# A two-layer transformer trunk in fp32: rsqrt and q/k scaling on GpSimd, the first k copies on ScalarE's queue, two preparations at other places

## The chip, the cores and the metric

One core of a Trainium2 chip runs the whole program. The time is the device time of one execution in microseconds (us), and what is compared is the median over runs. Five engines work from their own in-order instruction queues: TensorE (PE in the profile; its weight loads are PEld), VectorE (DVE), ScalarE (ACT), GpSimd (POOL) and SyncE (SP), which only starts transfers. ScalarE and GpSimd can start transfers too. Engines wait for one another through semaphores.

## The reference

The input is 512 tokens by 1024 features. Two layers follow one another, each an attention and a SwiGLU feed-forward, all with RMSNorm in front and a residual sum behind. The parts that matter here:

```python
def rms_norm(x, g):
    y = xf * lax.rsqrt(jnp.mean(xf * xf, axis=-1, keepdims=True) + EPS)
    return (y * g.astype(jnp.float32)).astype(x.dtype)

# layer 0: 16 heads of 64, strictly causal
z = einsum('bqhd,bkhd->bhqk', q_blk, k) * scale
log_keep = where(earlier, log_sigmoid(-z), 0.0)
log_after = lax.cumsum(log_keep, axis=3, reverse=True) - log_keep
weight = where(earlier, exp(log_sigmoid(z) + log_after), 0.0)

# layer 1: 8 heads, each with two query/key halves of 64 and values of 128
q = rms_norm(q.reshape(b, s, 8, 2, 64), q_g);  k = rms_norm(k.reshape(b, s, 8, 2, 64), k_g)
q1, q2, k1, k2 = partial_rope(..., positions)          # the first 16 of 64 features are rotated
lam = exp(sum(lq1 * lk1)) - exp(sum(lq2 * lk2)) + lam_init
a = softmax(q1 k1) - lam * softmax(q2 k2)               # block-causal
o = rms_norm(a @ v, sub_g) * (1.0 - lam_init)

# after either attention
x = x + einsum('bse,ed->bsd', o, w_out)
x = x + (silu(h @ w_gate) * (h @ w_up)) @ w_down        # h = rms_norm(x, ffn_norm), 2816 wide
```

Everything is float32 in and out.

## The kernel before, in words

**Products.** Every big product runs as three passes over a high and a low part (`mm3`, L215 to L218): high times high, high times low, low times high. A weight tile of 128x1024 is loaded by SP into a raw tile (two of them, tag "raw"), ScalarE rounds it to the high part `whi` (L109) and VectorE subtracts to get the low part `wlo` (L110). There are five pairs of such buffers. In layer 0 the low part is instead made by ScalarE (`wlo` = minus `whi`, L120) and an adding transfer that GpSimd starts (L121). Layer 1's weights are split once during the first feed-forward and kept in device memory (`keep_split`, L126 to L131, transfers started by GpSimd), and layer 1 reads them back (L133 to L137).

**Norms.** x lies transposed, as eight tiles of 128 features by 512 tokens. `Norm.scaled` (L157) makes `hhi` on ScalarE and `hlo` on VectorE from a tile of x and the gain; `Norm.square` (L167) squares the tile on ScalarE (`sq`) and adds it to `ssum` on VectorE (L177). `tile_done` does both when a tile of x is final. `finish` (L183) sums over partitions with four small matmuls into `ps_ss`, takes the inverse root with three Newton steps on VectorE (`rsqrt`, L139 to L149: one starting instruction, then three times three), and spreads it over partitions by a matmul into `ps_bc`, which ScalarE copies to `rbc`. The factor is applied after the products that use `hhi` and `hlo`.

**Layer 0** (`stick_layer`, L390). The first q and k (`pq`, `pk`) are projected at once. `stack_k` (L328) splits k into a high and a low part and copies each 64-partition half to the other half by a transfer that GpSimd starts (L334), because `scores` (L337) reads high and low stacked. `weights` (L484) takes two sigmoids on ScalarE from each score bank, a running product on VectorE (the scan, L494) and a multiply (L502); TensorE transposes the result (L358). While a pair of heads is worked on, the projections of the next pair and of v are fed in between as fillers. The output projection then adds its banks to x (L284, L298), and each finished x tile calls `tile_done` of the feed-forward's norm.

**Feed-forward** (`ffn`, L572). The 22 column tiles of gate and up are done in three portions, each followed by its part of the down projection, in PSUM banks of a pool of six and a pool of two. After the first portion's down projection the first feed-forward calls `setup_diff` (L627): eight and more small transfers started by SP, some 70 small VectorE instructions, and ScalarE's exponentials and sines for layer 1's rotation tables and lambda. These buffers come from a pool of their own, so they depend on nothing in the feed-forward.

**Layer 1** (`diff_layer`, L711). For each of four chunks (two heads each) `qk_steps` (L754) projects q and k of all tokens, squares them, takes an inverse root of 128x32 sums (L771), scales 128x2048 values on VectorE (L773) and rotates them on GpSimd (L790 to L793). `head_stacks` transposes (`tqk`) and stacks them. `weights` (L806) is a softmax pair joined by one VectorE instruction (L828). `head_out` (L851) normalises a head's output: two transposes (`tn`, `tb`), squares (`o_sq`, L865) and an inverse root of 128x4 sums (L876) between them, on VectorE.

**Order.** Each engine's order is not the order of the code: a scheduler runs a simulated timeline of the program and places every instruction on its engine when its operands would be ready there. A change of one instruction's engine or duration therefore also moves others.

## Time and profile before

| what | value |
|---|---|
| median of three runs | 1266.99 us (1265.03 to 1267.15) |
| profiled execution | 1268.86 us; its span from first to last instruction 1267.0 us |
| TensorE busy | 1225.4 us, 97% of the span |
| VectorE, ScalarE, GpSimd busy | 732.2, 566.8 and 101.4 us |
| idle time of TensorE | 41.6 us |
| mean granted TensorE clock | 0.990 |

Busy time is summed over the whole span, so an engine with a small share may still be the one that is waited for at one place. The granted clock is a share of full speed: 1.00 is TensorE's upper level (2.4 GHz), 0.50 its lower one (1.2 GHz). In rows of a timeline the brackets give the idle time before the instruction and what ended it.

### The profile page before, as it was taken

What the parts mean: (1) busy time and instruction counts of PE and PEld (TensorE: products, weight loads), DVE (VectorE), ACT (ScalarE), POOL (GpSimd) and SP (SyncE); (2) the same over time, 40 slices, a digit from 0 to 9 for tenths busy, and PEclk for the clock granted to TensorE, in tenths of its full rate; (3) what the DMA queues carried; (4) which work ended last, traced back from release to release, by engine and by line L of the source; (5) the groups of instructions that cost most, each with busy time, mean ns of one, the idle gap of its engine ahead of it and who ended that gap; (6) DMA issues with size and microseconds to landing.
All of it is one profiled execution on the core that took longest, in us unless ns stands there. A gap on an engine that the chain in (4) does not pass through costs nothing.

```text
span 1267.0 us, 16005 instructions
## 1 busy us (share of the span) xinstructions
PE 1225.4 (97%) x5974; PEld 1024.5 (81%) x5974; DVE 732.2 (58%) x1396; ACT 566.8 (45%) x962; POOL 101.4 (8%) x169
## 2 busy tenths in 40 slices
PE   7899999989999999999999999987999999999998
PEld 6788888768888888888888998775888888888886
DVE  6467777677654555455633777885754434443442
ACT  7687977555432333233423555554442222222320
POOL 2211112001111111001101201100000000000000
PEclk9899999999999999999999999999999999999999
DMA  6966848236867776767645463531333233322222
GB/s 205 218 124 152 182 102 199 67 106 222 270 227 248 242 226 234 252 236 234 241 184 184 150 212 99 179 100 34 106 111 98 87 100 100 100 89 95 96 75 79
DMA packets 60397, 198.39 MB, mean 157 GB/s; under 512 B 8288, under 2 KB 9312, under 8 KB 60320
## 3 DMA queue, kind: packets, MB, share of 16 engines
q1 hardware_dynamic: 41760, 138.90, 34.3%
q0 software_dynamic: 18416, 58.47, 17.0%
q8 instruction: 47, 0.77, 0.2%
q14 instruction: 30, 0.25, 0.1%
q10 hardware_dynamic: 144, 0.01, 0.0%
HBM read 153.31 MB, written 35.65 MB: 149 GB/s over the span
## 4 chain that ended last, share of the span: by engine, by line
PE 89%; DVE 3%; issue 3%; DMA 3%; ACT 1%; POOL 0%; SPq 0%; DVEq 0%; POOLq 0%; ACTq 0%
PE ps_d L216 6%; PE ps_d L217 6%; PE ps_d L218 6%; PE ps_u L216 6%; PE ps_g L216 6%; PE ps_u L218 6%; PE ps_g L217 6%; PE ps_u L217 6%; PE ps_g L218 6%; PE ps_nat L216 4%; PE ps_nat L217 4%; PE ps_nat L218 4%; PE ps_o L216 2%; PE ps_o L217 2%; PE ps_o L218 2%
## 5 line engine op out<-in xcount | busy, mean ns | idle before, releaser
L109 ACT ACTIVATE whi<-wraw 128x1024 fp32r<-128x1024 f32 (+1 forms) x138 | 140.6, 1034 | 344.2 <-PE ps_d L217 82.4
L110 DVE TENSOR_TENSOR wlo<-wraw,whi 128x1024 fp32r<-128x1024 f32 (+1 forms) x138 | 164.2, 1191 | 93.7 <-ACT whi L109 47.5
L216 PE MATMUL ps_u<-hhi,whi 128*128 128x512 f32 x352 | 137.9, 392 | 3.5 <-DVE k L679 3.5
L217 PE MATMUL ps_d<-alo,whi 128*128 128x512 f32 x352 | 138.9, 396 | 0.0
L218 PE MATMUL ps_d<-ahi,wlo 128*128 128x512 f32 x352 | 138.9, 396 | 0.0
L216 PE MATMUL ps_d<-ahi,whi 128*128 128x512 f32 x352 | 138.7, 396 | 0.0
L216 PE MATMUL ps_g<-hhi,whi 128*128 128x512 f32 x352 | 137.5, 392 | 0.0
L218 PE MATMUL ps_u<-hhi,wlo 128*128 128x512 f32 x352 | 137.3, 390 | 0.0
L218 PE MATMUL ps_g<-hhi,wlo 128*128 128x512 f32 x352 | 137.2, 390 | 0.0
L217 PE MATMUL ps_g<-hlo,whi 128*128 128x512 f32 x352 | 137.1, 390 | 0.0
L217 PE MATMUL ps_u<-hlo,whi 128*128 128x512 f32 x352 | 137.0, 390 | 0.0
L216 PE MATMUL ps_nat<-whi,hhi 128*128 128x256 f32 (+1 forms) x384 | 124.1, 324 | 3.6 <-DVE k L457 3.0
L218 PE MATMUL ps_nat<-whi,hlo 128*128 128x256 f32 (+1 forms) x384 | 123.5, 322 | 0.0
L217 PE MATMUL ps_nat<-wlo,hhi 128*128 128x256 f32 (+1 forms) x384 | 122.9, 321 | 0.0
L610 DVE TENSOR_TENSOR x<-x,ps_d 128x512 f32<-128x512 f32 x48 | 32.8, 686 | 100.2 <-PE ps_d L218 100.2
L216 PEld LDWEIGHTS ps_nat<-whi,hhi 128*128 128x128 f32 x384 | 72.7, 190 | 11.0 <-DVE k L457 3.5
L216 PEld LDWEIGHTS ps_u<-hhi,whi 128*128 128x128 f32 x352 | 66.4, 189 | 17.9 <-issue 4.1
L218 PEld LDWEIGHTS ps_d<-ahi,wlo 128*128 128x128 f32 x352 | 66.1, 188 | 16.0
L216 PEld LDWEIGHTS ps_d<-ahi,whi 128*128 128x128 f32 x352 | 66.1, 188 | 16.0
L217 PEld LDWEIGHTS ps_d<-alo,whi 128*128 128x128 f32 x352 | 66.1, 188 | 15.9
L216 PEld LDWEIGHTS ps_g<-hhi,whi 128*128 128x128 f32 x352 | 66.4, 189 | 14.1 <-issue 0.2
L217 PEld LDWEIGHTS ps_g<-hlo,whi 128*128 128x128 f32 x352 | 66.2, 188 | 14.0 <-issue 0.2
(207 smaller groups left out, 2335.7 us busy)
## 6 DMA issues: line engine op xcount, KB each, us to landing
wraw<-in_wgu SPq DMA_DIRECT2D x88, 512.0 KB, 3.5
wraw<-in_wd SPq DMA_DIRECT2D x32, 512.0 KB, 3.6
k<-k POOLq DMA_DIRECT2D x32, 256.0 KB, 4.4
praw<-in_wqk SPq DMA_DIRECT2D x16, 512.0 KB, 5.1
kept_wqk<-whi POOLq DMA_DIRECT2D x16, 512.0 KB, 4.4
kept_wqk<-wlo POOLq DMA_DIRECT2D x16, 512.0 KB, 6.0
whi<-kept_wqk SPq DMA_DIRECT2D x16, 512.0 KB, 6.3
wlo<-kept_wqk SPq DMA_DIRECT2D x16, 512.0 KB, 6.2
```

What stands on the lines that cost most here:

```text
L109: A.activation(hi[:, :cols], raw[:, :cols], AF.Copy)
L110: V.tensor_tensor(lo[:, :cols], raw[:, :cols], hi.bitcast(F32)[:, :cols], op=ALU.subtract)
L216: T.matmul(ps, lh[0], rh[0], start=first, stop=False)
L217: T.matmul(ps, lh[0], rh[1], start=False, stop=False)
L218: T.matmul(ps, lh[1], rh[0], start=False, stop=last)
L610: V.tensor_tensor(x[m], x[m], ps, op=ALU.add)
```

## The change

Five edits:

1. The Newton steps of layer 1's inverse roots run on GpSimd (`rsqrt_pool`): the starting instruction stays on VectorE, and 13 GpSimd instructions follow, since each step takes four there instead of three. It is used for the q/k norm of all four chunks and for `head_out` of the first seven heads; the last head keeps VectorE (`final`). With it, two small multiplies per head move as well.
2. The 128x2048 scaling of q and k moves from VectorE (L773) to GpSimd (after: L810).
3. The first k copies of layer 0 are started from ScalarE's queue instead of GpSimd's.
4. The two feed-forward norms square their tiles only after the eighth tile is done, and the seven additions into `ssum` run on GpSimd (`early=False`).
5. `setup_diff` takes its buffers from a raw tile of the feed-forward's pool, which ties it to that pool's other users.

```diff
+    def rsqrt_pool(v, n):
...
+        V.tensor_scalar(
+            u.bitcast(I32), v.bitcast(I32), -0.5, RSQRT_MAGIC, op0=ALU.mult, op1=ALU.add
+        )
+        G.tensor_tensor(v, v, half.to_broadcast([P, n]), op=ALU.mult)
+        for _ in range(3):
+            G.tensor_tensor(t, u, u, op=ALU.mult)
+            G.tensor_tensor(t, t, v, op=ALU.mult)
+            G.tensor_tensor(t, t, c15.to_broadcast([P, n]), op=ALU.add)
+            G.tensor_tensor(u, t, u, op=ALU.mult)
+        return u
...
-        def square(self, i, eng=None):
+        def square(self, i, eng=None, add=V):
...
-                V.tensor_tensor(self.s, self.s, sq, op=ALU.add)
+                add.tensor_tensor(self.s, self.s, sq, op=ALU.add)
...
         def tile_done(self, i):
             self.scaled(i)
-            self.square(i)
+            if self.early:
+                self.square(i)
+            elif i == KT - 1:
+                for j in range(KT):
+                    self.square(j, None, G)
...
-            G.dma_start(out=k2[o, :, e], in_=k2[r, :, e])
+            q.dma_start(out=k2.bitcast(F32)[o, :, e], in_=k2.bitcast(F32)[r, :, e])
...
-            k2 = k_stack(pk)
+            k2 = k_stack(pk, A)
...
-                    side[0]()
+                    side[0](rawp)
...
+        sp = Scratch(pool.tile([P, 1024], F32, tag="raw", name="setup"))
...
-                u = rsqrt(ss, 32)
+                u = rsqrt_pool(ss, 32)
...
-                V.tensor_tensor(
+                G.tensor_tensor(
                     f3, f3, u.unsqueeze(2).to_broadcast([P, 32, 64]), op=ALU.mult
...
+                E = V if final else G
+                E.tensor_tensor(fin, fin, rs, op=ALU.mult)
...
+                u = (rsqrt if final else rsqrt_pool)(v, TT)
+                E.tensor_tensor(u, u, fin, op=ALU.mult)
...
-    n1 = Norm(gf, 0, True)
+    n1 = Norm(gf, 0, True, False)
...
-    n3 = Norm(gf, KT, True)
+    n3 = Norm(gf, KT, True, False)
```

Where instructions stand on the engines, at three places. First GpSimd's queue in layer 0, before, from the first adding weight transfers on; k_323 is the first stacked k, k_592 that of the next pair of heads:

```order
L121 DMA wlo<-in_wqk 128x1024 x2
L121 DMA wlo<-in_wv 128x1024
L334 DMA k_323<-k_323 64x2x512 x2
L121 DMA wlo<-in_wv 128x1024
L121 DMA wlo<-in_wqk 128x1024 x3
L334 DMA k_592<-k_592 64x2x512 x2
```

After, the same engine and place, where the copies of the first k are gone and k_596 is the next pair's:

```order
L121 DMA wlo<-in_wqk 128x1024 x2
L121 DMA wlo<-in_wv 128x1024 x2
L121 DMA wlo<-in_wqk 128x1024 x3
L357 DMA k_596<-k_596 64x2x512 x2
```

The two copies now stand on ScalarE, behind the split of k and one evacuation of v (k_327 is the first stacked k there):

```order
L334 ACTIVATE k_327<-k_325 64x512 x2
L457 ACTIVATE v_338<-ps_nat,rstd 128x4x64
L357 DMA k_327<-k_327 64x2x512 x2
L119 ACTIVATE whi<-wraw 128x1024
L457 ACTIVATE v_338<-ps_nat,rstd 128x4x64
L119 ACTIVATE whi<-wraw 128x1024
```

So the first k copies no longer share GpSimd's queue with the adding weight transfers, and an instruction of ScalarE precedes the next weight's rounding.

Second, VectorE at the end of layer 0's output projection, before: x_78 to x_85 are the tiles of x, pf, gqT, la and r belong to `setup_diff`:

```order
L537 TENSOR_TENSOR olo<-o_2336,ohi 128x512
L668 CAST pf<-pi 128x4
L298 TENSOR_TENSOR x_78<-x_78,ps_o 128x512
L674 TENSOR_SCALAR r<-pf 128x4 x3
L298 TENSOR_TENSOR x_79<-x_79,ps_o 128x512
L641 TENSOR_TENSOR gqT<-gqT,gkT 128x1
L674 TENSOR_SCALAR r<-pf 128x4 x3
L652 TENSOR_TENSOR la_3805<-la_3805,lb_3806 128x64
L674 TENSOR_SCALAR r<-pf 128x4
L298 TENSOR_TENSOR x_80<-x_80,ps_o 128x512
```

After, the same place:

```order
L560 TENSOR_TENSOR olo<-o_2340,ohi 128x512
L321 TENSOR_TENSOR x_78<-x_78,ps_o 128x512
L321 TENSOR_TENSOR x_79<-x_79,ps_o 128x512
L321 TENSOR_TENSOR x_80<-x_80,ps_o 128x512
L321 TENSOR_TENSOR x_81<-x_81,ps_o 128x512
L110 TENSOR_TENSOR wlo<-wraw,whi 128x1024
L321 TENSOR_TENSOR x_82<-x_82,ps_o 128x512
L181 SCALAR_TENSOR_TENSOR hlo<-x_78,gf,hhi 128x512
L321 TENSOR_TENSOR x_83<-x_83,ps_o 128x512
L110 TENSOR_TENSOR wlo<-wraw,whi 128x1024
L181 SCALAR_TENSOR_TENSOR hlo<-x_79,gf,hhi 128x512
```

The instructions of `setup_diff`, and with them the waits for its transfers, have left this place and stand behind the down projection of the first portion; the `ssum` additions have left VectorE.

Third, GpSimd in layer 1 after, around the second chunk's scaling (rs_u is the inverse root, k_6142 and k_6494 stacked k of two heads); before, only the rotation and the copies stood there:

```order
L167 TENSOR_TENSOR rs_u<-rs_t,rs_u 128x32
L810 TENSOR_TENSOR qk_nat<-qk_nat,rs_u 128x2048
L357 DMA k_6142<-k_6142 64x2x512 x2
L827 TENSOR_TENSOR rope<-qk_nat,rot_105 128x16x8
L828 TENSOR_TENSOR rope<-qk_nat,rot_105 128x16x8
L829 TENSOR_TENSOR rope<-qk_nat,rot_104 128x256
L827 TENSOR_TENSOR rope<-qk_nat,rot_107 128x16x8
L828 TENSOR_TENSOR rope<-qk_nat,rot_107 128x16x8
L829 TENSOR_TENSOR rope<-qk_nat,rot_106 128x256
L830 TENSOR_TENSOR qk_nat<-rope 128x4x4x16 x2
L357 DMA k_6494<-k_6494 64x2x512 x2
L912 TENSOR_TENSOR fin<-fin,rs_6410 128x4
```

The copy of a stacked k now stands behind a chunk's scaling on the same queue.

## Rows read from the trace of the kernel before

**Rows 1.** Page, busy time of each engine: us, share, instructions.

```profile
PE 1225.4 (97%) x5974; PEld 1024.5 (81%) x5974; DVE 732.2 (58%) x1396; ACT 566.8 (45%) x962; POOL 101.4 (8%) x169
```

**Rows 2.** Timeline, PE, first scores: start, us, instruction, [idle before, releaser].

```profile
40.66 0.39 PE L218 MATMUL ps_q<-hhi,wlo 128*128 128x512 f32 x1
...
45.42 0.77 PE L340 MATMUL sc<-k,q 128*128 128x512 f32 x1 [4.36 <-DMA k<-k]
...
55.41 0.71 PE L358 MATMUL tp<-ident,w 128*128 128x128 f32 x5
```

**Rows 3.** Timeline, POOL, ACT and DVE, 33 to 52 us.

```profile
33.59 1.33 POOL L334 DMA_DIRECT2D k<-k  x2 [0.37 <-DVE k L312]
44.88 1.06 ACT L119 ACTIVATE whi<-wraw 128x1024 fp32r<-128x1024 f32 x1 [2.96 <-DMA wraw<-in_wqk]
47.72 0.69 ACT L491 ACTIVATE keep<-sc,rn 128x512 f32<-128x512 f32 x1
51.43 0.56 DVE L502 TENSOR_TENSOR w<-w,qq 128x384 f32<-128x384 f32 x1
```

**Rows 4.** Page, DMA issues: queue, count, KB each, median us to landing.

```profile
k<-k POOLq DMA_DIRECT2D x32, 256.0 KB, 4.4
```

**Rows 5.** Windows: length, busy PE PEld DVE ACT POOL, clock, DMA share, GB/s.

```profile
33.00:46.00 13.00, 8.52 (x45) 6.78 (x44) 1.95 (x4) 6.43 (x9) 3.29 (x5) 0.94 1.11 249
46.00:51.30 5.30, 5.30 (x16) 4.37 (x15) 3.44 (x4) 5.25 (x8) 0.13 (x1) 0.51 0.96 276
269.50:275.00 5.50, 5.46 (x17) 4.40 (x18) 5.50 (x11) 4.29 (x8) 0.00 (x0) 0.69 0.35 133
660.00:800.00 140.00, 139.74 (x869) 125.34 (x869) 92.17 (x268) 71.41 (x180) 20.80 (x36) 1.00 0.55 178
800.00:872.00 72.00, 63.47 (x334) 51.69 (x333) 61.46 (x216) 37.99 (x116) 6.88 (x12) 0.95 0.29 92
895.00:930.00 35.00, 35.00 (x158) 28.70 (x157) 25.40 (x45) 16.77 (x23) 0.00 (x0) 1.00 0.38 120
```

**Rows 6.** Timeline, DVE, ACT and PE, layer 0 into the first feed-forward.

```profile
259.28 0.17 DVE L668 CAST pf<-pi 128x4 f32<-128x4 int32 x1 [2.37 <-DMA pi<-in_pos]
...
264.34 0.23 DVE L652 TENSOR_TENSOR la<-la,lb 128x64 f32<-128x64 f32 x1 [0.94 <-DMA lb<-in_lk]
268.71 0.68 DVE L298 TENSOR_TENSOR x<-x,ps_o 128x512 f32<-128x512 f32 x1
267.26 1.28 ACT L655 ACT_TABLE_LOAD   x1
269.54 0.64 PE L216 MATMUL ps_u<-hhi,whi 128*128 128x512 f32 x1 [3.48 <-DVE k L679]
```

**Rows 7.** Groups by line and shape, 640:930 (POOL: whole span): busy, mean ns, idle.

```profile
L773 DVE TENSOR_TENSOR qk_nat<-qk_nat,rs_u 128x2048 f32<-128x2048 f32 x4 | 9.2, 2288 | 0.1
L177 DVE TENSOR_TENSOR ssum<-ssum,sq 128x512 f32<-128x512 f32 x7 | 4.8, 687 | 0.2
L146 DVE SCALAR_TENSOR_TENSOR rs_t<-rs_u 128x4 f32<-128x4 f32 x30 | 4.7, 156 | 0.5
L791 POOL TENSOR_TENSOR rope<-qk_nat,rot 128x128 f32<-128x128 f32 x8 | 3.9, 485 | 0.0
L792 POOL TENSOR_TENSOR rope<-qk_nat,rot 128x256 f32<-128x256 f32 x8 | 5.8, 729 | 0.0
```

**Rows 8.** Timeline, DVE's joining of the two softmaxes, and POOL's rotation beside it.

```profile
818.19 1.44 POOL L793 TENSOR_TENSOR qk_nat<-rope 128x256 f32<-128x256 f32 x2
818.85 1.34 DVE L828 SCALAR_TENSOR_TENSOR e<-e,c,e 128x512 f32<-128x512 f32 x1
844.46 0.75 DVE L828 SCALAR_TENSOR_TENSOR e<-e,c,e 128x512 f32<-128x512 f32 x1
```

**Rows 9.** Timeline, ACT and PE, the last head of layer 1.

```profile
878.92 1.06 ACT L109 ACTIVATE whi<-wraw 128x1024 fp32r<-128x1024 f32 x1 [2.93 <-DMA wraw<-in_wgu]
885.02 1.09 PE L887 MATMUL tb<-ident,wraw 128*128 128x128 f32 x4 [4.13 <-DVE wraw L878]
```

## What the change will do, predicted before it ran

> **What bounds the kernel now.** I read the share of each engine first: TensorE is busy for 1225.4 of 1267.0 us [rows 1], so 41.6 us is all that can be had from idle time, and the question is only where those microseconds lie. TensorE's timeline puts them in five places: 6.4 us at the start and 3.9 at the end (neither touched by the change), one wait of 4.36 us before the first scores [rows 2], one of 3.48 us at the first feed-forward [rows 6], and the last part of layer 1, where TensorE is busy for 63.47 of 72 us [rows 5] and then waits 4.13 us for the last head [rows 9]. After a wait TensorE also runs at a lower granted clock for a while: 0.51 in the 5.3 us after the first wait, 0.69 in the 5.5 us after the second [rows 5]. Elsewhere, between 660 and 800 us above all, it is busy for 139.74 of 140 us [rows 5]: there the change can only cost. Each edit is weighed at the place where it acts.
>
> **First k copies from ScalarE's queue.** GpSimd starts them at 33.59 [rows 3]. They land 11.69 us later, at about 45.3: the scores wait for them until 45.42 [rows 2]. The usual landing is 4.4 us after issue [rows 4]. Both the queue, which they share with adding weight transfers, and full DMA engines (share 1.11 between 33 and 46 us, [rows 5]) can be the reason; moving them removes only the first. If it works, the scores come up to 4.36 us earlier, at 41.06. What is late next? The sigmoids stand on ScalarE behind a weight's rounding that waits for its own load until 44.88 [rows 3], so the first sigmoid stays near 47.7 [rows 3]. TensorE goes on with the k projection, which needs neither, and then wants to transpose. The transposes at 55.41 [rows 2] need two finished rows of weights, the second of which ends on VectorE at 51.43 + 0.56 = 51.99 [rows 3]. So they can move from 55.41 to 52.0, 3.4 us. I take **-3.4**. The ends are 0 (full engines, the copies no earlier) and -7.0: the whole wait, 4.36, and the clock, since 16 matmuls filled 5.30 us at 0.51 and at full clock half of it, 2.6, would do [rows 5].
>
> **Preparation and squares at the first feed-forward.** Before, three waits of VectorE for tiny transfers, the first of 2.37 and the last of 0.94 us [rows 6], stand in its queue among the additions into x, and ScalarE loads an activation table for 1.28 us in the middle of the `hhi` instructions [rows 6]. The sixth addition ends at 268.71 + 0.68 = 269.39, and TensorE starts at 269.54 [rows 6], so that addition, not the releaser named in the row, ended the wait. After, the additions follow one another and the table load is gone. I leave 0.5 of the 3.48 us: 3.0 gained. The clock: 17 matmuls in 5.5 us are 0.32 each, where the second feed-forward's first 35.00 us at clock 1.00 hold 158, 0.22 each [rows 5], so 17 x 0.10 = 1.7 more. Together -4.7.
>
> Against it stand the seven additions that move to GpSimd. A GpSimd instruction of 128x128 takes 485 ns and one of 128x256 takes 729 [rows 7]; continued in a straight line (an estimate), 128x512 takes about 1.2 us, against 0.687 on VectorE [rows 7]. Seven are 8.5 us, and ScalarE's squares wait for them, since their buffers number three, and the later `hhi` stand behind those squares in ScalarE's order. They also lie beside VectorE's `hlo` and `wlo`. The one pair of rows that shows what happens there: an instruction of VectorE with two inputs took 1.34 us beside GpSimd's rotation and 0.75 without it [rows 8], 0.59 more. If three of the eleven `hlo` and `wlo` are hit on the path, 3 x 0.59 = 1.8 us come back. I take -4.7 + 1.8 = **-2.9**; the ends are -4.7 and +1.8 (all eleven hit: 6.5 back).
>
> The Trainium skill ("SBUF — State Buffer", section "Who interferes with whom") speaks against this edit: VectorE's second port pair is GpSimd's only one, held as an exclusive lock. The 1.34 us agrees in kind. By the rule at its full strength each addition would hold a two-input instruction for its own 1.2 us, and the edit would give nothing; that is a rival below.
>
> **The same squares at the second feed-forward.** Here TensorE has no idle time to win: 35.00 of 35 us at clock 1.00 [rows 5]. VectorE loses seven additions, 4.8 us [rows 7], but was busy for only 25.4 of 35 [rows 5], so nothing is gained. The same three hits cost 3 x 0.59: **+1.8**, ends 0 and +3.5 (six hits).
>
> **Newton and scaling off VectorE, end of layer 1.** Between 800 and 872 us VectorE is busy for 61.46 of 72 us [rows 5] and TensorE idles for 8.5. What leaves VectorE: one scaling, 2.29 us [rows 7]; nine steps of 128x32 and four heads with nine steps of 128x4 each, 45 x 0.156 = 7.0 us [rows 7], and two small multiplies a head. That is over 9 us. What comes: per head 13 GpSimd instructions in a row, about 0.25 us each by the same line, 3.2 us against 1.4 on VectorE; so each head's second transpose comes 1.8 us later by itself, with other heads' work between. And the scaling on GpSimd, 128x2048 by the line (0.0019 us an element and 0.24), is 4.1 us long, in which VectorE's joining of the softmaxes can be held. I let the scaling count as nothing and take half of the idle time, **-4**; ends -8.5 and +1.8 x 3 = +5.4 (the heads' chain unhidden three times).
>
> **The last head.** It keeps VectorE. TensorE waits 4.13 us for it, and in that chain a weight's rounding that had waited 2.93 us for its load holds ScalarE for 1.06 us before the squares [rows 9]. The load's raw tile is one that a head used; in the new order the seventh head's second transpose stands before the eighth's values product, so the tile is free earlier and the rounding out of the way: **-1.5**, ends 0 and -2.9.
>
> **The full stretch before it.** Between 660 and 800 us three chunks get their Newton and scaling on GpSimd. Each chain is longer by 13 x 0.30 + 4.1 - (9 x 0.16 + 2.29) = 4.3 us, and the copy of a stacked k now stands behind the scaling in the same queue. TensorE's fillers cover most. I take **+1.5** for the reshuffled order, ends 0 and 3 x 4.3 = +12.9.
>
> **At nothing.** The preparation inside the feed-forward is hidden by VectorE's slack there (58% busy over the span, [rows 1]) and five weight buffers; it holds one of two raw tiles of the kept weights, and costs perhaps 2 us if those fall behind. The two small constants are set beside the start's loads.
>
> **Sum.** -3.4 - 2.9 + 1.8 - 4 - 1.5 + 1.5 = -8.5. The profiled execution took 1268.86 us, 1.87 above the median 1266.99; 1268.86 - 8.5 = 1260.4, and for the median 1258.5.
>
> **Rivals.** (1) The ports do not matter, and the lighter VectorE frees most of the last stretch: -3.4 - 4.7 + 0 - 6 - 1.5 + 0 = -15.6, 1251.4 us. For it: GpSimd is busy 8% only [rows 1]. Against: the 0.59 us of [rows 8].
> (2) GpSimd holds VectorE for whole instructions: both feed-forward starts lose their gain (0 and +3.5), the scaling undoes the relief in layer 1 (0): -3.4 + 0 + 3.5 + 0 - 1.5 + 1.5 = +0.1, no change, 1267 us. For it: [rows 8]. Against: that row lost 0.59, not the 1.44 of the two rotations. It is the skill's lock taken literally, named above.
> (3) Slower: GpSimd's queue in layer 1 becomes the bound. Rotation and k copies behind Newton and scaling come 4.3 us later per chunk in a stretch where TensorE has nothing to spare; with all three unhidden, 12.9 in place of the 1.5 (+11.4), and the relief in the last stretch at 0 (+4): -8.5 + 11.4 + 4 = +6.9, 1274 us. It ends slower than before once more than about 2 us per chunk stay uncovered: 3 x 2 in place of 1.5 makes -8.5 + 4.5 + 4 = 0. For it: in the new order the copy of a k stands directly behind the scaling. Against: the order of TensorE was made for these times, with fillers put before the transposes.
> (4) The copies come no earlier, for the DMA engines were full (1.11, [rows 5]): the first term is 0, 1261.9 us.
>
> **How the numbers follow.** Forecast 0.50, own range 1252 to 1264; rival (1) 0.17; (2) 0.12; (3) 0.13; (4) 0.08. About 0.2%, 2.5 us, is what a measurement of this kernel can tell from no change. Faster by more than that (under 1264.5) are nearly all of the forecast, (1), most of (4) and a little of (2): 0.48 + 0.17 + 0.07 + 0.02 = 0.74. No change are the rest of these, 0.02 + 0.01 + 0.10 = 0.13; slower is (3), 0.13. The range reaches from below (1) to between (2) and (3): 1249 to 1268.
>
> **What would show it.** Right: scores at about 41 us and the first transposes at about 52; additions into x without a wait for small transfers, and the first feed-forward's start without 3 us of idle time; `hlo` of some 1.3 us beside GpSimd's additions; VectorE under 54 us busy in the stretch before the last head. Wrong: k copies landing at 45 again; a wait of TensorE for the transposed q and k of a chunk (`tqk`) or for a k copy between 660 and 800 us; `ssum` ending so late that the first gate product's banks fill up; a new wait in the first feed-forward for a raw tile. The forecast falls if the stretch from 660 to 800 us grows by more than 4 us.

## The result: slower by half a per cent

The changed kernel took 1273.14 us (median of six runs, 1269.66 to 1274.75) against 1266.01 us before: a ratio of 1.0055 with a 95% interval of 1.0041 to 1.0069, some 7 us slower. Forecast were 1258.5 us, in a range that ended at 1268.

The profiled execution of the changed kernel, 1269.66 us, is the fastest of its six, and the profiled one of before, 1268.86, is longer than every other execution of that kernel on record (1262.25 to 1268.53). So the two profiles differ by far less than the medians, and they are read here by stage. From the timelines of TensorE, the start of the same instruction in each kernel (us from the start of the span; the third is the changed kernel in a second profiled execution):

| instruction of TensorE | before | changed | changed, again |
|---|---|---|---|
| first scores | 45.42 | 42.64 | 43.98 |
| first transpose of the weights | 55.41 | 51.61 | 54.15 |
| first product of the first feed-forward | 269.54 | 266.02 | 266.21 |
| last product of the first feed-forward | 635.49 | 631.21 | 631.37 |
| first scores of layer 1 | 690.43 | 694.28 | 694.01 |
| first product of the second feed-forward | 898.42 | 898.69 | 900.30 |
| last product | 1262.66 | 1263.63 | 1264.89 |

Up to the end of the first feed-forward the changed kernel is ahead by 4.3 us; forecast were 6.3 up to there (3.4 and 2.9). Layer 1 then takes 898.69 - 631.21 = 267.5 us, and 268.9 in the second execution, where it took 262.9 before. The whole gain goes there. Windows of the changed kernel over the stretches of [rows 5] (columns as there; the second lies around the start of the first feed-forward):

```profile
46.00:51.30 5.30, 4.19 (x18) 3.04 (x17) 2.43 (x3) 5.27 (x8) 0.00 (x0) 1.00 1.03 238
262.40:268.00 5.60, 5.59 (x25) 4.32 (x23) 5.60 (x5) 5.50 (x10) 5.27 (x4) 1.00 0.40 105
660.00:800.00 140.00, 135.67 (x821) 119.54 (x820) 78.48 (x196) 66.73 (x167) 47.14 (x113) 1.00 0.49 163
800.00:872.00 72.00, 64.59 (x349) 52.58 (x347) 57.81 (x168) 40.73 (x128) 28.66 (x88) 0.98 0.30 96
896.00:931.00 35.00, 34.75 (x155) 27.96 (x154) 27.80 (x41) 18.69 (x26) 10.25 (x6) 1.00 0.35 117
```

The 3.5 us of idle time of [rows 6] and the lower clock of [rows 5] are gone from the first feed-forward's start (5.59 of 5.60 us busy at clock 1.00). But the stretch from 660 to 800 us, full before, now has 4.3 us without work, with VectorE relieved by 13.7 us (78.48 for 92.17) and GpSimd busy for 47.14 us instead of 20.80. So VectorE's load was not what was short there. What TensorE waited for in layer 1, in its timeline and that of GpSimd and in the chain of work that ended last (the third row: start, us from issue to landing):

```profile
694.28 0.50 PE L363 MATMUL sc<-k,q 128*128 128x512 f32 x1 [2.06 <-DMA k<-k]
686.25 1.36 POOL L357 DMA_DIRECT2D k<-k  x2 [16.60 <-DVE qk_ss L800]
686.25 7.99 DMA k<-k
...
748.58 0.66 PE L897 MATMUL tn<-ident,wraw 128*128 128x128 f32 x4 [0.71 <-ACT wraw L891]
793.23 0.66 PE L925 MATMUL tb<-ident,wraw 128*128 128x128 f32 x4 [0.65 <-DVE wraw L916]
794.81 0.50 PE L363 MATMUL sc<-k,q 128*128 128x512 f32 x1 [0.69 <-DMA k<-k]
885.37 1.09 PE L925 MATMUL tb<-ident,wraw 128*128 128x128 f32 x4 [5.18 <-DVE wraw L916]
```

The copy of the first stacked k of layer 1 leaves GpSimd's queue without delay by the scaling (GpSimd had been idle for 16.60 us), but lands only 7.99 us after its start; [rows 4] had 4.4. The longest wait, 5.18 us for the last head, was 4.13 us before [rows 9]; the others are short. In all TensorE is without work for 18.0 us of layer 1 here (from the last product of the first feed-forward to the first of the second) and was for 14.6 us before.

GpSimd's own durations and VectorE's beside them, groups by line and shape between 640 and 930 us (columns as in [rows 7]):

```profile
L810 POOL TENSOR_TENSOR qk_nat<-qk_nat,rs_u 128x2048 f32<-128x2048 f32 x4 | 14.5, 3628 | 0.3
L196 POOL TENSOR_TENSOR ssum<-ssum,sq 128x512 f32<-128x512 f32 x7 | 11.5, 1650 | 25.6 <-ACT sq L192 25.3
L165 POOL TENSOR_TENSOR rs_t<-rs_t,o_ss 128x4 f32<-128x4 f32 x21 | 4.8, 228 | 1.6
L181 DVE SCALAR_TENSOR_TENSOR hlo<-x,gf,hhi 128x512 fp32r<-128x512 f32 x8 | 9.3, 1196 | 0.0
```

The scaling takes 3.63 us (4.1 was estimated, 2.29 on VectorE), an addition 1.65 (1.2 estimated, 0.69 on VectorE).

### The profile page after: what moved, and what is told of

It reads as the page before. It is cut to its first block, busy times and chain, and to the rows that moved or that the text cites. A ratio compares the mean times of both kernels' runs of the same rounds, so it can differ in the third digit from the quotient of the medians.

```text
span 1267.9 us, 16075 instructions
## 1 busy us (share of the span) xinstructions
PE 1225.3 (97%) x5974; PEld 1021.4 (81%) x5974; DVE 719.3 (57%) x1267; ACT 565.1 (45%) x963; POOL 174.0 (14%) x342
## 4 chain that ended last, share of the span: by engine, by line
PE 83%; DVE 5%; DMA 4%; ACT 3%; issue 3%; POOL 1%; SPq 0%; DVEq 0%; POOLq 0%; ACTq 0%
PE ps_d L240 6%; PE ps_d L241 6%; PE ps_d L239 6%; PE ps_g L240 6%; PE ps_u L240 6%; PE ps_u L241 6%; PE ps_g L241 6%; PE ps_u L239 6%; PE ps_g L239 6%; PE ps_nat L239 3%; PE ps_nat L240 3%; PE ps_nat L241 3%; PE ps_o L239 2%; PE ps_o L240 2%; PE ps_o L241 2%
## 5 line engine op out<-in xcount | busy, mean ns | idle before, releaser
L110 DVE TENSOR_TENSOR wlo<-wraw,whi 128x1024 fp32r<-128x1024 f32 (+1 forms) x138 | 166.9, 1210 | 104.9 <-ACT whi L109 48.4
L240 PEld LDWEIGHTS ps_u<-hlo,whi 128*128 128x128 f32 x352 | 66.1, 188 | 14.6 <-DVE hlo L181 1.0
```

What stands on the lines that cost most here:

```text
L110: V.tensor_tensor(lo[:, :cols], raw[:, :cols], hi.bitcast(F32)[:, :cols], op=ALU.subtract)
L240: T.matmul(ps, lh[0], rh[1], start=False, stop=False)
```

## The experiments

Each kernel ran in five rounds beside the kernel before; the medians of before in these batches were 1265.2 to 1265.7 us. Intervals are those of the ratio to before.

**The changed kernel again** (no edit). 

> The changed kernel itself, unchanged, to see where a second execution loses time: its profiled execution (1269.66 us) was the fastest of six, the others lay between 1272.9 and 1274.8. If the missing 3 us are chance in the granted clock after short waits, the second profile shows the same waits of TensorE (first scores of layer 1 about 2 us, a head's second transpose about 0.7 us in the full stretch) and a lower mean clock than 0.994; if they come from another wait, a wait stands there that the first profile lacks. Time 1273 us.

Measured: 1274.42 us, ratio 1.0077 (1.0059 to 1.0096). The second profile has the same waits (first scores of layer 1, second transposes) at a mean clock of 0.990 against 0.994, and the wait for the second k copy is longer (1.53 us for 0.69). It is the third column of the table above. Both profiles are the fastest of their six executions (the other five here took 1273.16 to 1279.15 us), so neither can show where the slower ones lose their time. What is on record for each of those is the mean clock, 0.985 in the one of 1279.15 us. Over all 126 executions of the changed kernel and the kernels below, 0.001 less of mean clock goes with 0.76 us more within the same kernel (a straight line through the differences from each kernel's own mean; correlation -0.77).

**Layer 1's edits undone.**

```diff
-                u = rsqrt_pool(ss, 32)
+                u = rsqrt(ss, 32)
-                G.tensor_tensor(
+                V.tensor_tensor(
                     f3, f3, u.unsqueeze(2).to_broadcast([P, 32, 64]), op=ALU.mult
-                E = V if final else G
+                E = V
-                u = (rsqrt if final else rsqrt_pool)(v, TT)
+                u = rsqrt(v, TT)
```

> Newton steps and scaling of layer 1 back on VectorE; the k copies on ScalarE's queue, the later preparation and the late squares on GpSimd stay. Theory 1 (layer 1's chains on GpSimd cost the time): the gains up to the end of the first feed-forward, 4.3 us in the profile, stay, and layer 1 is as before: 1262 us. Rival (the squares on GpSimd hold VectorE back at both feed-forward starts, or the later preparation costs): 1268 us or more.

Measured: 1260.66 us, 0.9966 (0.9952 to 0.9979). Theory 1 holds: the three edits outside layer 1 make the kernel 4.9 us faster than before, those in layer 1 make it 13.8 us slower than that (1274.42 - 1260.66). Layer 1 takes 259.7 us here, 13.4 of them without work for TensorE. The executions have a median clock of 0.994, the changed kernel's beside them one of 0.989: by the line above some 4 of the 13.8 us go with the lower clock (an estimate).

**Only the scaling back on VectorE** (the second pair of lines above). 

> Only the 128x2048 scaling back on VectorE, the Newton steps stay on GpSimd. If the scaling is the cost (3.6 us on GpSimd against 2.3, and it holds VectorE's instructions with two inputs): 1266 us or less. If the Newton chains are (13 instructions of 0.28 us pitch, 3.6 us against 1.4 on VectorE, in front of each head's second transpose): 1271 to 1273 us.

Measured: 1269.88 us, 1.0040 (1.0026 to 1.0053): 4.5 us won, in between the two expectations.

**Squares and their additions as before** (`n1` and `n3` without the last `False`). 

> Only the squares of the two feed-forward norms as before (after each tile, added on VectorE). If GpSimd's additions hold up the low parts at the starts of the feed-forwards, some 2 to 4 us are won: 1270 us. Theory 1 says they do not matter: the profile shows 0.7 us lost at the second start and 4.3 won at the first: 1273 us, within 1.5.

Measured: 1272.06 us, 1.0059 (1.0036 to 1.0082), within the spread of the changed kernel. It does not decide between the two expectations. From first to last product the two feed-forwards take 364.24 and 364.23 us here, in the changed kernel 365.19 and 364.94.

The next three add one edit of layer 1 each to the run without them.

**Newton of the heads on GpSimd** (the last two pairs of lines restored). 

> As the run without layer 1's edits (1260.7 us), with the Newton steps of the first seven heads' output norm on GpSimd. Theory 1 in detail: the chain in front of each head's second transpose grows by over 2 us and shows as late transposes in the full stretch and at the end of layer 1; of the 9.2 us that the two Newton edits cost together some 5 are here: 1265 to 1266 us. Rival (the heads' chain is hidden by the fillers and the cost lies in the chunks): 1261 us.

Measured: 1266.63 us, 1.0006 (0.9995 to 1.0017): 6.0 us lost, as expected in size. The reason given, a longer chain, is not what the profile shows. From the first instruction behind the sums to the end of the scaled output, head 4, where the difference is largest, takes on VectorE (the kernel with k copies and preparation alone) and with the steps on GpSimd:

```profile
793.37 0.22 DVE L910 TENSOR_SCALAR fin<-o_ss,thr 128x4 f32<-128x4 f32 x1
802.89 0.68 DVE L916 TENSOR_TENSOR wraw<-tn,rs_u 128x512 f32<-128x512 f32 x1
```

```profile
794.63 0.23 DVE L910 TENSOR_SCALAR fin<-o_ss,thr 128x4 f32<-128x4 f32 x1 [0.85 <-ACT o_sq L902]
799.73 0.68 DVE L916 TENSOR_TENSOR wraw<-tn,rs_u 128x512 f32<-128x512 f32 x1
```

That is 10.2 us on VectorE, where other work stands between the steps, and 5.8 on GpSimd, where nothing does. Over the first seven heads it is 5.0 to 10.2 us on VectorE, 6.9 on average, and 5.3 to 6.4 us on GpSimd, 5.7 on average; at two of the seven it is longer on GpSimd, by 0.3 us each. So the chain did not grow on average. What grew are waits elsewhere. TensorE waits 2.6 us for k copies in layer 1 (0.88, 0.47 and 1.28), where the base does not wait for any. And it waits longer for the last head, whose steps stayed on VectorE; in the run without layer 1's edits and in this one:

```profile
879.26 0.63 PE L925 MATMUL tb<-ident,wraw 128*128 128x128 f32 x4 [4.07 <-DVE wraw L916]
```

```profile
879.83 1.09 PE L925 MATMUL tb<-ident,wraw 128*128 128x128 f32 x4 [6.39 <-DVE wraw L916]
```

In the base some 3 us of the output projection stand between that head's two transposes on TensorE; in the new order they all come before the first, and nothing is left to fill the wait.

**Newton of the chunks on GpSimd** (the first pair restored). 

> As the run without layer 1's edits (1260.7 us), with the Newton steps of the four chunks' q/k norm on GpSimd and the scaling on VectorE. If the new order that comes with the longer chain puts the first chunk's k copy beside the weight reloads, the first scores wait about 2 us for it as in the changed kernel: 1263 us, up to 1265. If that wait needs the scaling on GpSimd too: 1261 us.

Measured: 1268.12 us, 1.0020 (1.0011 to 1.0029): 7.5 us lost, more than either expectation; the wait for the first k copy is there (1.49 us). From the sums to the end of the rotation the four chunks take 11.5, 12.6, 13.3 and 14.1 us in its profile, where they take 10.2, 12.9, 11.3 and 14.4 in the base's: two of the four are even shorter, so this chain's length alone does not explain the loss.

**The scaling on GpSimd alone.** 

> As the run without layer 1's edits (1260.7 us), with only the 128x2048 scaling on GpSimd. Undoing it alone won 4.5 us; if the edits add up it costs 4 to 5 alone: 1265 us. If it costs only together with the Newton steps on the same queue (k copies and head chains behind it): within 1.5 us of 1260.7.

Measured: 1276.47 us, 1.0084 (1.0071 to 1.0097): 15.8 us lost, more than all three edits together. The rows show one reason. Timelines of GpSimd, VectorE, ScalarE and TensorE in this run:

```profile
810.48 3.62 POOL L810 TENSOR_TENSOR qk_nat<-qk_nat,rs_u 128x2048 f32<-128x2048 f32 x1 [12.55 <-DVE c L861]
811.64 3.00 DVE L865 SCALAR_TENSOR_TENSOR e<-e,c,e 128x512 f32<-128x512 f32 x1
815.21 0.58 ACT L853 ACTIVATE e<-sc,nm 128x384 f32<-128x384 f32 x1 [3.06 <-DVE nm L852]
815.93 0.38 PE L363 MATMUL sc<-k,q 128*128 128x256 f32 x1 [2.57 <-ACT e L853]
```

The joining of the softmaxes, 0.75 us alone [rows 8], starts while GpSimd scales and ends at 814.64, half a microsecond after GpSimd's end at 814.10: it stood still. The maximum behind it on VectorE is late, so is the exponential on ScalarE, and TensorE finds no free bank for the scores. At the second and third chunk the same instruction took 4.15 and 2.92 us on shapes that take 0.6 and 0.35. The Trainium skill ("SBUF — State Buffer", section "Who interferes with whom") says that a VectorE instruction with two SBUF inputs contends with a GpSimd instruction that reads SBUF, that what they share is an exclusive lock, and that the order of issue decides which of the two is blocked. These rows agree, to half a microsecond, that the one stands still until the other ends. On the order they say less: at the second chunk the joining's start on record lies 0.09 us before the scaling's (699.07 and 699.16), and it was the joining that stood still.

The waits are not the whole loss. Windows over layer 1, in the run without its edits and in this one:

```profile
632.06:891.71 259.65, 246.21 (x1403) 211.81 (x1401) 173.89 (x531) 127.04 (x327) 31.30 (x51) 0.99 0.42 140
```

```profile
628.23:904.66 276.43, 253.78 (x1403) 216.83 (x1401) 172.47 (x526) 126.99 (x328) 47.55 (x56) 0.96 0.39 131
```

TensorE has 22.65 us without work for 13.44, 9.2 more. And it is busy at the lower clock level for 19.8 us of layer 1 instead of 6.2; half of the difference, 6.8 us, is what the lower level costs (an estimate). Together that is 16.0 of the 16.8 us by which layer 1 is longer.

**The scaling on GpSimd in four pieces.**

```diff
+                for i in range(4):
+                    g8 = slice(i * 8, i * 8 + 8)
+                    G.tensor_tensor(
+                        f3[:, g8], f3[:, g8], u[:, g8].unsqueeze(2).to_broadcast([P, 8, 64]), op=ALU.mult
+                    )
```

> As the run with only the scaling on GpSimd (1276.5 us), in four instructions of 128x512 instead of one of 128x2048. If the one long instruction of 3.6 us costs because a two-input instruction of VectorE beside it stands still until it ends (the joining of the softmaxes took 4.15, 2.92 and 3.00 us there instead of 0.6, 0.3 and 0.75), the stop is at most some 1 us now and 3 to 6 us come back: 1270 to 1273 us. If the latency of the chain or the new order costs: 1276 us or more.

Measured: 1268.75 us, 1.0032 (1.0020 to 1.0044): 7.7 us come back. TensorE's waits for the exponentials of layer 1, by the view of waits (us in total, times, longest), with one piece, with four, and with the scaling on VectorE (k copies and preparation alone):

```profile
PE sc L363 <- ACT e L853: 10.1, 9, 2.6
```

```profile
PE sc L363 <- ACT e L855: 4.5, 8, 1.3
```

```profile
PE sc L363 <- ACT e L853: 3.0, 3, 1.8
```

So 7.1 us of the 15.8 are this wait, and 5.6 of them go with the long instruction. What the joinings of layer 1 take beyond the 0.75, 0.60, 0.47 or 0.35 us that is usual for their shape adds up to 9.4 us with one piece, 2.6 with four, and 1.1 without layer 1's edits. So the standstill is shown as a cause. How much of the 7.7 us is its own was not separated, since the cut changed the order too (TensorE has another instruction at 898 of 5974 places); the clock of layer 1 rose with it, from 0.96 to 0.97.

**The same four pieces in the changed kernel.** 

> The changed kernel with the scaling in four instructions of 128x512 on GpSimd. If the holding of VectorE by the one long instruction is what the scaling costs there too (two joinings of the softmaxes held by 2.7 and 1.3 us in the profile): 1269 to 1270 us, as with the scaling on VectorE (1269.9). If it is the order: anything between 1266 and 1276.

Measured: 1271.73 us, 1.0046 (1.0031 to 1.0062), 1.4 us below the changed kernel's first median and 2.7 below its second, with intervals that overlap: less than expected, and not to be told from no change. With the Newton steps on GpSimd as well, the order has other instructions beside the scaling. In the changed kernel's profile two joinings were held, but only one of them beside the scaling, by 1.3 us. The other was held by 2.7 us beside the rotation, where GpSimd ran five short instructions one right behind the other (VectorE, then GpSimd; in the second profile that joining takes 3.48 us too):

```profile
703.84 3.48 DVE L865 SCALAR_TENSOR_TENSOR e<-e,c,e 128x512 f32<-128x512 f32 x1
...
703.82 0.46 POOL L827 TENSOR_TENSOR rope<-qk_nat,rot 128x128 f32<-128x128 f32 x1
704.24 0.45 POOL L828 TENSOR_TENSOR rope<-qk_nat,rot 128x128 f32<-128x128 f32 x1
704.65 0.73 POOL L829 TENSOR_TENSOR rope<-qk_nat,rot 128x256 f32<-128x256 f32 x1
705.35 1.41 POOL L830 TENSOR_TENSOR qk_nat<-rope 128x256 f32<-128x256 f32 x2
```

Cutting the scaling could not touch that one. It also shows that short instructions alone do not bound the wait: VectorE's instruction ended only behind the fifth (707.32 and 706.76).

**First k copies and preparation alone** (all of layer 1 and the squares as before). 

> Only the first k copies from ScalarE's queue and the later preparation; squares as before, all of layer 1 on VectorE. If the late squares on GpSimd win nothing at the first feed-forward and cost 0.7 us at the second, as the profiles read: 1260 us. If they are what lets the first feed-forward start without a wait: 1263 us.

Measured: 1259.73 us, 0.9949 (0.9937 to 0.9961). By the medians the late squares on GpSimd cost 0.9 us, which the intervals do not tell from nothing; by the profiles the first feed-forward takes 364.24 us from first to last product where it took 365.14 with them, the second 364.23 where it took 364.97.

**First k copies alone.** 

> The kernel before with one edit: the first k copies of layer 0 from ScalarE's queue. The two together with the later preparation won 5.8 us (1259.7 against 1265.5). By the profiles the first scores come 2.8 to 3.8 us earlier and 1.5 to 4.5 us of that are left at 100 us: 1263 us, between 1261 and 1264.

Measured: 1264.60 us, 0.9997 (0.9987 to 1.0006): nothing that can be told from no change, against an expected 2 and outside the stated range. The scores wait 1.39 us for the copies in its profile instead of 4.36. The copies land 8.6 and 10.0 us after their issue from ScalarE's queue, against 11.7 and 11.9 before and the usual 4.4 of [rows 4]: more than half of the delay was not GpSimd's queue.

**Preparation alone.** 

> The kernel before with one edit: the preparation of layer 1 in a raw tile of the first feed-forward. By the profiles the wait of 3.5 us at the first feed-forward goes, with the lower clock behind it: 1262 us, between 1261 and 1263. Both edits then add up to the 5.8 us.

Measured: 1260.04 us, 0.9965 (0.9953 to 0.9977): 5.2 us, more than the 2 to 4 expected. Nearly the whole gain is this edit; with the 0.6 us of the copies it adds up to the 5.8 of both. In this profile the copies are still on GpSimd's queue, and the first scores start at 43.97 after a wait of 3.49 us, 0.9 less than in [rows 2] with the same queue: single executions differ by that much.

**Squares late, added on VectorE.**

```diff
-                    self.square(j, None, G)
+                    self.square(j)
```

> As the run with k copies and preparation alone (1259.7 us), with the feed-forward squares after the eighth tile, but added on VectorE. With the additions on GpSimd it took 1260.7 us, with six of VectorE's two-input instructions held at each start, 5.6 us in all. If that holding reaches TensorE: 1259.5 us here; if lateness itself costs (the inverse root later than the first products): 1261 us; at most 1.5 us between them, so a tie is likely.

Measured: 1260.02 us, 0.9954 (0.9942 to 0.9967): the tie, 0.6 us from the additions on GpSimd. These are the rows of the standstill at the first feed-forward's start in the changed kernel, VectorE and GpSimd:

```profile
262.64 1.69 DVE L181 SCALAR_TENSOR_TENSOR hlo<-x,gf,hhi 128x512 fp32r<-128x512 f32 x1
264.85 1.72 DVE L110 TENSOR_TENSOR wlo<-wraw,whi 128x1024 fp32r<-128x1024 f32 x1
266.50 1.78 DVE L181 SCALAR_TENSOR_TENSOR hlo<-x,gf,hhi 128x512 fp32r<-128x512 f32 x1
...
262.49 10.35 POOL L196 TENSOR_TENSOR ssum<-ssum,sq 128x512 f32<-128x512 f32 x6 [37.55 <-ACT sq L192]
```

`hlo` takes 1.7 us where 0.74 is usual, and seven of VectorE's instructions are held for 5.6 us in all; yet TensorE waited 0.34 us here, once. The stops are many here and cost little. The first feed-forward takes 365.19 us from first to last product in the changed kernel and 364.24 with the additions on VectorE: 0.95 us, in that wait and in others too short to be listed, beside products that read `hlo`. That so little came of 5.6 us may be because seven additions (4.8 us, [rows 7]) had left VectorE; no run separates it.

**The 13 Newton instructions behind the starting one, on VectorE** (the chunks' steps in the form of `rsqrt_pool`, with V for G; added to k copies and preparation). 

> As the run with k copies and preparation alone (1259.7 us), with the chunks' Newton steps in the 13 instructions of the GpSimd version, but on VectorE: no work on another engine, only a chain longer by 3 short instructions and whatever new order follows from it. Theory 2: layer 1 is full and its order is fitted to its chains, so that a new order alone costs several us, as the GpSimd versions did (7.5 us for this Newton): 1264 us or more. Rival (it is GpSimd itself, its chain, its ports or its queue): within 1.5 us of 1259.7.

Measured: 1266.86 us, 1.0017 (1.0008 to 1.0026): 7.1 us lost with nothing on another engine, about as much as the same steps on GpSimd cost (7.5). From the sums to the end of the rotation the second chunk takes (k copies and preparation alone, then with 13 instructions):

```profile
690.77 0.18 DVE L807 TENSOR_SCALAR qk_ss<-qk_ss 128x32 f32<-128x32 f32 x1
702.27 1.43 POOL L830 TENSOR_TENSOR qk_nat<-rope 128x256 f32<-128x256 f32 x2
```

```profile
688.25 0.18 DVE L821 TENSOR_SCALAR qk_ss<-qk_ss 128x32 f32<-128x32 f32 x1
704.37 1.61 POOL L844 TENSOR_TENSOR qk_nat<-rope 128x256 f32<-128x256 f32 x2
```

12.9 us became 17.7, though four instructions of under 0.2 us were added (13 for 9 behind the starting one; the expectation counts three): the new order has more of the other work between the steps. The other three chunks became longer by 1.5, 2.9 and 3.0 us.

**Two Newton steps instead of three** (`rsqrt(ss, 32, 2)` in the chunks, the loop over `range(steps)`; added to k copies and preparation). 

> As the run with k copies and preparation alone (1259.7 us), with two Newton steps instead of three in the q/k norm of the four chunks, on VectorE: three instructions less in each chunk's chain (this leaves out a third of the refinement). Less work, a shorter chain, nothing on another engine, but another order. Theory 2 (a new order alone costs): 1262 us or more. Rival (the length of the chain decides): 1259.7 or less.

Measured: 1257.80 us, 0.9932 (0.9920 to 0.9944), 1.9 us faster. This leaves out the last step of the refinement. Some 330 of 5675 rows of TensorE's timeline stand elsewhere, so a new order need not cost. Theory 2 falls in the form it was written; the shorter chain and the new order are not separated here either.

**Three idle copies per chunk.**

```diff
+                nd = sm.tile([P, 2], F32, tag="nd", bufs=1, name="nd")
+                for _ in range(3):
+                    V.tensor_copy(nd, norm.rstd[:, 0:2])
```

> As the run with k copies and preparation alone (1259.7 us), with three copies of 128x2 values per chunk on VectorE (under 0.2 us each, 2 us in all) that nothing waits for. The order of TensorE changes in layer 1, no chain becomes longer. Theory 2 (a new order alone costs several us): 1262 us or more. Rival: the 2 us of work disappear in VectorE's idle time, 1260 us.

Measured: 1253.29 us, 0.9904 (0.9890 to 0.9918): 6.4 us faster than its base, with more work. It does not test theory 2 at all, because TensorE's order turned out the same row for row; the expectation was wrong in that. The gain lies in the down projections, which nothing had touched: each feed-forward takes 360.7 us where it took 364.2. By the addresses in the compiled programs the tile `nd` takes 32 bytes of each partition, and what is allocated behind it, `ahi` and `alo` among it, lies 32 bytes further. In the kernels before it the tiles of x, h and the weights begin 32 bytes past a multiple of 64 and `ahi` and `alo` at one; now all begin 32 past. Two runs were made to find out.

**8 unused bytes behind the weights' tiles.**

```diff
+    pad = sm.tile([P, 2], F32, tag="pad", bufs=1, name="pad")
+    nc.vector.memset(pad, 0.0)
```

> As the run with k copies and preparation alone (1259.7 us), with 8 more bytes per partition in the pool of small tiles, cleared once and never used: every tile allocated behind it, the feed-forward's ahi and alo among them, lies 32 bytes further, the weights' tiles do not. The order of TensorE is the same row for row. In the run with the three idle copies the down projection's matmuls came every 0.2267 us instead of 0.2333, 1056 of them. If the place of the tiles does that: 1253 us, down projection at 0.2267. If the copies did it: 1259.7 us.

Measured: 1251.48 us, 0.9892 (0.9876 to 0.9908), the fastest kernel of all: 13.7 us below the kernel before. The groups of the down projection between 300 and 630 us, before the shift (k copies and preparation alone) and after it:

```profile
L239 PE MATMUL ps_d<-ahi,whi 128*128 128x512 f32 x176 | 69.5, 396 | 0.0
L239 PE MATMUL ps_u<-hhi,whi 128*128 128x512 f32 x152 | 59.1, 389 | 0.0
```

```profile
L241 PE MATMUL ps_d<-ahi,whi 128*128 128x512 f32 x176 | 68.3, 389 | 0.0
L241 PE MATMUL ps_u<-hhi,whi 128*128 128x512 f32 x152 | 59.1, 389 | 0.0
```

And the window of 30 us inside it, before and after the shift:

```profile
360.00:390.00 30.00, 30.00 (x130) 24.18 (x129) 19.45 (x80) 11.63 (x15) 2.32 (x5) 1.00 0.60 195
```

```profile
360.00:390.00 30.00, 30.00 (x134) 24.86 (x133) 20.28 (x92) 10.86 (x15) 2.65 (x5) 1.00 0.55 184
```

TensorE is busy without a gap at clock 1.00 in both, and does 134 matmuls instead of 130. The mean distance of the down projection's matmuls in the timelines is 0.2333 us and 0.2267 us; 1056 of them make 7.0 us, of 8.3 between the two medians.

**4 unused bytes in front of all tiles** (the same with the pool of constants). 

> As the run with k copies and preparation alone (1259.7 us), with 4 more bytes per partition in the pool of constants: all tiles of x, h and the weights and those of the feed-forward lie 32 bytes further. If the down projection is slow where its weights and its moving tiles lie differently to a multiple of 64 bytes: gate and up stay at 0.2267 us, down stays at 0.2333, 1260 us. If a moving tile that begins at a multiple of 64 is slow by itself: gate and up (moving tiles at a multiple of 64 now) go to 0.2333, down (no longer) to 0.2267: 1253 + 2112 x 0.0067 = 1267 us.

Measured: 1260.19 us, 0.9960 (0.9947 to 0.9972), down projection at 0.2333, gate and up at 0.2267. Now the moving tiles of gate and up begin at a multiple of 64 bytes and those of the down projection do not, and nothing changes. So it is not the place of one tile, but whether the weights' tiles and the moving tiles lie alike or differently to a multiple of 64 bytes. Only the places 0 and 32 were tried.

## Why the prediction was wrong, point by point

**The step that failed: layer 1, in three terms.** I wrote of the end of layer 1 "I let the scaling count as nothing and take half of the idle time, -4", of the stretch before it "TensorE's fillers cover most", +1.5, and of the last head -1.5: -4 in all. The runs put +13.8 us there. The relief of VectorE that I counted is there in part (61.46 us busy fell to 57.81 between 800 and 872 us, where under 54 was expected) but was not what the stage needed: TensorE waits there for exponentials, k copies, transposed weights and scaled outputs in turn, which suggests that the time of a step in the order counted more than an engine's load. The sign named beforehand for a wrong forecast came: a wait for a k copy in layer 1 (2.06 us at 694.28), and 4.3 us without work between 660 and 800 us. In the profiles layer 1 loses in two ways, by idle time of TensorE (18.0 us, and 13.4 without layer 1's edits) and by a lower clock; the second was in no term for layer 1.

- *The scaling* alone costs 15.8 us. The waits for exponentials behind VectorE's standstill are 7.1 of them, and 5.6 go when it is cut in four; idle time and lower clock together are 16.0. I had the mechanism in hand, as the rival with GpSimd holding VectorE for whole instructions. In the sum I let the scaling count as nothing, and in that rival it only undid the relief of 4 us; the one price I had was the 0.59 us of [rows 8]. That row did not bound it: GpSimd's instructions there were two of 0.72 us, so the wait could hardly have been longer.
- *The heads' chain* I priced as longer on GpSimd by counting instructions (13 x 0.25 against 9 x 0.156 us). It is shorter there on average (5.7 us against 6.9 over seven heads), since on VectorE the steps stand among other work. The edit costs 6.0 us all the same.
- *The chunks' chain* costs 7.5 us, and about as much, 7.1, with the same 13 instructions on VectorE. So neither GpSimd nor a port is needed for such a price; that the two losses have one cause is not shown. I had each chain longer by 4.3 us; from the sums to the end of the rotation it is longer by 1.9 us on average in the changed kernel (12.8, 14.7, 14.0 and 15.0 us for 10.2, 12.9, 11.2 and 14.4).
- *The last head* was to wait 1.5 us less and waits 1.05 us more (5.18 for 4.13). The weight's rounding did get out of the way, as I wrote: it runs at 875.96, before the head's squares at 880.23. But the new order also put the products of the output projection that had filled the wait before that head's first transpose, and nothing stands between the two.

The rival that came out, by time, is the slower one (1274 us, chance 0.13). By mechanism only half of it did: k copies do land late (7.99 and 7.65 us after issue), but the first of them not because of the queue, since GpSimd had been idle for 16.60 us; it lands beside the reloads of weights, with a DMA share of 0.89 between 686.0 and 694.3 us.

**First k copies, -3.4.** Measured -0.6, within the noise. The wait goes down, to between 1.05 and 2.74 us in the profiles with this edit, though the copies still land late. The bound that I took, two finished rows of weights, was not one: in the changed kernel the first transpose starts at 51.61, behind the first row (51.47), while the second ends at 53.00. But the sum was made on one execution that was late there; against the profile of the preparation alone, with the copies on GpSimd, the scores of the two edits together come 2.3 us earlier (41.67 for 43.97), and their medians are 0.3 us apart. In these two profiles the gain is gone by the start of the first feed-forward (264.52 for 263.42), with TensorE's order the same: from the first scores on, the mean clock is 0.985 in the one with both edits, 0.992 in the other.

**Preparation and squares, -2.9 and +1.8.** The preparation brought 5.2 us, above the end of 4.7 that I gave. The squares' price at both starts is 0.6 to 0.9 us by the medians and 1.6 by the lengths of the feed-forwards, not 3.6: at the first, hits were seven, not three, each of some 0.8 us, not 0.59, and little of it was on the path. Two errors that partly cancelled.

**Preparation inside the feed-forward, nothing.** Right: no wait for a raw tile appears.

**What stays open.** Alone the three edits of layer 1 cost 6.0, 7.5 and 15.8 us, together 13.8. Of the scaling's price the waits behind the standstill are 5.6 to 7.1 us and the lower clock some 6.8 (an estimate). For the Newton steps, the runs show that four dependent instructions more lose 7.1 us and three fewer win 1.9, each with a new order of all engines; how much is the longer chain and how much the order that the scheduler makes from it was not separated, since no order could be held fixed while a duration changed.

## What to carry to other kernels

Where TensorE is full and several engines pass short steps around a ring, the load of one engine says little: price a move by the time from its first input to its last output in the order that results, treat a moved chain as a new schedule, and look at what is left to fill the waits. Short waits cost more than their length where the granted clock is lower behind them. Before a long instruction is put on GpSimd, look for two-input instructions of VectorE that will start beside it, and price them at the whole length of GpSimd's instruction. In pieces it cost 7.7 us less here, but several short ones in a row held VectorE for 2.7 us as well. And read the distance between matmuls of products that nobody changed: a small tile added somewhere may have moved their operands. Last, take more than one profile of a kernel before a sum is made on it: the one of the kernel before was its slowest execution.

## What the runs showed of the hardware that was not expected

- The place of tiles sets the pace of matmuls: with the weights' tiles and the moving tiles at the same place relative to a multiple of 64 bytes a 128x512 matmul comes every 0.2267 us, otherwise every 0.2333 us, 2.9% more, at the same clock of 1.00. In the kernel before all down projections are of the second kind, 7 us.
- GpSimd's 128x512 addition takes 1.65 us beside VectorE's work, and an instruction of 128x4 0.22 to 0.23, where one of VectorE's takes 0.16 [rows 7].
- The same idle time of 1.46 us at the same transposes of layer 0 is followed by a full clock in one execution and by a lower one in another of the same kernel. Windows of the changed kernel right behind that wait, in its second and its first profile (28 and 20 matmuls in the same busy time):

```profile
238.00:244.00 6.00, 5.55 (x28) 4.28 (x27) 4.23 (x9) 3.05 (x7) 0.00 (x0) 1.00 0.00 0
```

```profile
238.00:244.00 6.00, 5.55 (x20) 4.15 (x19) 3.96 (x9) 2.93 (x7) 0.00 (x0) 0.72 0.00 0
```

0.72 is a mix of the two levels of 1.2 and 2.4 GHz. Steps of this kind fit the spread of single executions of one kernel, 0.9 to 10.7 us, in which the longer ones have the lower mean clock; a sum made on one profile carries that much error.
